# The RWKV stage of a two-stream transformer kernel, with full-width masks, chunks taken by pairs of heads and double buffers

## Chip, cores and metric

The kernel runs on one core of a Trainium2 chip. The time is device microseconds (us) of one execution; lower is better.

## What is computed

The reference runs four transformer layers over a latent and a context stream, 256 tokens of 1024 features each. The first layer's mixer is half attention, half RWKV-7: a linear recurrence for 8 heads of 64, forward (`d` = 0) and backward (`d` = 1) in time, the latent stream starting from the state that the context stream left. Cut to what matters:

```python
kk = kk * lax.rsqrt(jnp.sum(kk * kk, axis=-1, keepdims=True) + EPS)
w_log = w0 + einsum('btdr,drc->btdc', tanh(wl), w2)            # low rank, 64
decay = exp(-exp(-softplus(-w_log) - 0.5))
a = sigmoid(a0 + einsum('btdr,drc->btdc', al, a2))             # low rank, 64
def step(S, inp):
    r, w, k, v, kk, a = inp
    S = (S * w[:, :, None, :]
         - einsum('bhvk,bhk->bhv', S, kk)[..., None] * (kk * a)[:, :, None, :]
         + v[..., None] * k[:, :, None, :])
    return S, einsum('bhvk,bhk->bhv', S, r)
S_cf, y_cf = wkv7_scan(S0, dir_inputs(f_ctx, 0), reverse=False)
_, y_lf = wkv7_scan(S_cf, dir_inputs(f_lat, 0), reverse=False)   # and both backward
```

## The kernel before, in words

Activations lie feature-major: 128 features on the partitions, tokens along the free axis. Big products split each operand in a high and a low fp32r part and take three matmuls (`mm3`, L137); small products are plain fp32. All records of a matmul carry the line of the helper `mm` (L107), so places are told by tile names: `lin` and `aux` are PSUM tiles of big products and attention, `rw` those of the RWKV stage. A scheduler places instructions on each engine's queue in the order that it expects them to become ready, with the order of the code as priority; engines then run their queues in order. PSUM's eight banks are shared by the tags of `BANKS` (L28), which caps `rw` at 5.

The recurrence is done in chunks of 64 tokens (four per stream) and pairs of heads (`hp`, four). Class `Rwkv` (from L878) has, for one stream, generators that yield at their seams: `keys` (key norms and the bonus term), `front` (per pair `features`, then `scores`), `inverse` (a triangular inverse for all pairs at once), `mid` (`chunks`, per pair and per two chunks), `steps` (the state recurrence) and `readout`. `even_mixer` (L702) makes A for the context stream and B for the latent one, and `weave` runs them side by side: A.front with B.keys, A.inverse with the start of B.front, A.mid and A.steps with the rest of it, then A.readout with B.inverse, B.mid, B.steps, B.readout. The output projections (`half_out_proj`) fill in between: `oa` is the attention half, `ob` the RWKV half.

What the change touches:
- `features` (L923): two low rank products of K = 128 and 512 columns (`lowa`, zero-padded so that both directions fit one product), tanh on ScalarE (`FL`, `SA`), then a chain on VectorE with a scan (L941).
- `scores` (L962): transposes of v and Qt (L971, L979); per direction 8 products `ZW`x`SA` into [128, 4, 128], then eight masks on 64 partitions, half into `AL` and half into `BL`; then the products of `BL` and `KV`; then the transposes of `SA` (L1015), copied to `ZW` and `KV` (L1016, L1017); then `KV` products, copied to `Cc` (L1026). `KV` and `BL` have one buffer.
- `chunks` (L1138): 8 products `QV`x`AL`, a copy and a negating copy (L1148 and the next), 28 products, subtractions and additions on VectorE.

```python
                for hf, ps in enumerate(pss):
                    for dst, sr in ((AL[dr, :, hf], slice(0, 64)), (BL[dr, :, hf], slice(64, 128))):
                        m = self.smask[sr, d, None, :].to_broadcast([64, 4, P])
                        self.last_score = k.mul(dst, ps[sr], m)
```

Of the kernel before, what the change touches and what calls it, by code (L numbers as in the profile page):

```python
# [11 lines left out]
AF = mybir.ActivationFunctionType  # L12
# [3 lines left out]
P = 128  # L16
KC = 8
NS = 256
# [9 lines left out]
BANKS = {"lin": 4, "aux": 4, "mod": 1, "rw": 5}  # L28
# [674 lines left out]
def even_mixer(k, nm, gate, nxt):  # L703
# [3 lines left out]
    low = {("gl", s): k.t([P, NS], "low", 1) for s in range(2)}  # L707
    for n in ("wl", "al"):
        for s in range(2):
            low[n, s] = k.t([P, 2, NS], "lowa", 2)  # L710
            for d in range(2):
                k.after(nc.gpsimd.memset(low[n, s][64 - 64 * d:128 - 64 * d, d], 0.0), k.mark)
# [35 lines left out]
    def features():  # L748
        for idx in range(6, 21):
# [4 lines left out]
            for st in sts:  # L754
                if name[0] in "rkv":
                    t = T[name, st.s] = k.t([P, NS], f"rkv{st.s}", 3)
                elif name == "gl":
                    t = low[name, st.s]
                else:
                    t = k.r([P, NS], "s1")  # L760
# [4 lines left out]
                if name in ("wl", "al"):  # L765
                    for d in range(2):
                        dr = slice(64 * d, 64 * d + 64)
                        k.act(low[name, st.s][dr, d], t[dr], AF.Tanh if name == "wl" else AF.Copy)
# [110 lines left out]
class Rwkv:  # L879
# [3 lines left out]
    def __init__(self, k, st, T, low, lora, hb, gw, PCs, msk, before=None):  # L883
        self.k, self.st, self.T, self.low, self.lora, self.hb = k, st, T, low, lora, hb
        self.gw, self.PC, self.before = gw, PCs[st.s], before
        self.rmask, self.smask = msk[:, 0:512], msk[:, 512:768].rearrange("p (d t) -> p d t", d=2)
# [5 lines left out]
    def keys(self):  # L892
# [4 lines left out]
        for hp in range(4):  # L897
            r_, k_, v_ = (T[f"{n}{hp}", st.s] for n in "rkv")
            a = k.r([P, NS], "s1")
            k.stt(a, r_, k.v("r_k", hp), k_, ALU.mult, ALU.mult)  # L900
            pb = rw((P, NS))
            k.mm(pb, k.bd, a, True, True)
            k.mul(bon[:, hp], pb, v_)
            b = k.r([P, NS], "s1")
            k.ts(b, k_, k.v("k_k", hp), ALU.mult, -1.0, ALU.mult)
            sq = k.r([P, NS], "s1")
            k.act(sq, b, AF.Square)
            rr = head_rstd(k, sq, NS, 1.0, 1e-6, "rw")
            k.mul(kks[:, hp], b, rr)
            yield  # L910

    def front(self, early):
# [5 lines left out]
        self.Cc = [k.t([P, 2, 4, 64], "Cc", 4) for _ in range(4)]  # L918
# [3 lines left out]
        def features(hp):  # L922
# [7 lines left out]
            for i, (w, x) in enumerate(((w2, "wl"), (a2, "al"))):  # L930
                pw = rw((P, 2, NS))
                k.mm(pw.rearrange("p d t -> p (d t)"), w[:, cs],
                     self.low[x, st.s].rearrange("p d t -> p (d t)"), True, True)
                for d in range(2):
                    b = 8 * i + 4 * d + hp
                    k.act((SG, A)[i][:, :, d], pw[:, d].rearrange("p (c t) -> p c t", c=4), AF.Tanh, scale=0.5,
# [25 lines left out]
        def scores(hp):  # L962
# [4 lines left out]
            KV = k.t([P, 2, 4, P], "KV", 1)  # L967
# [15 lines left out]
            BL = k.t([P, 4, 2, P], "BL", 1)  # L983
            for d in range(2):
# [6 lines left out]
                for hf, ps in enumerate(pss):  # L991
                    for dst, sr in ((AL[dr, :, hf], slice(0, 64)), (BL[dr, :, hf], slice(64, 128))):
                        m = self.smask[sr, d, None, :].to_broadcast([64, 4, P])
                        self.last_score = k.mul(dst, ps[sr], m)
                yield
            for c in (0, 2):
# [13 lines left out]
                nc.scalar.copy(self.Y[:, hp, 64 * c:64 * c + 128], py.rearrange("p c t -> p (c t)"))  # L1010
            for d in range(2):
# [779 lines left out]
```

## Time and profile before

| | |
|---|---|
| runs | 3443.32 us median of 3 (3440.03 to 3454.67) |
| profiled execution | 3438.3 us, its span 3436.5 us |
| busy | TensorE 94%, VectorE 69%, ScalarE 43% of the span |
| mean granted TensorE clock | 0.961 |
| RWKV stage (about 593 to 953 us in the span) | granted clock 0.59 to 0.83 |

Shares over the whole span say little here: the stage that is changed has its own limits, so it is read by stretches, by the chain of waits within it, and by the timelines of single engines.

### The profile page before, as it was taken

How to read it: one execution, taken by the hardware profiler on the slowest of the kernel's cores; microseconds unless marked ns; L12 is line 12 of the kernel's file. 1: busy time of each engine (PE TensorE's matmuls, PEld its weight loads, DVE VectorE, ACT ScalarE, POOL GpSimd, SP SyncE). 2: the span in 40 equal slices, each digit the busy share in tenths (PEclk: the TensorE clock that was granted, in tenths of full speed). 3: DMA queues.
4: the chain of work that ended last, by engine and by line, in shares of the span. 5: the costliest groups of instructions: out<-in, count | busy, mean ns of one | idle time of the engine just before them, and what ended most of it. 6: DMA issues, size and time to landing. Idle time of an engine off the chain costs nothing.

```text
span 3436.5 us, 51379 instructions
## 1 busy us (share of the span) xinstructions
PE 3239.4 (94%) x20538; PEld 2775.9 (81%) x20538; DVE 2367.3 (69%) x4452; ACT 1489.2 (43%) x2611; POOL 7.1 (0%) x20
## 2 busy tenths in 40 slices
PE   8999989657689999999988999999999999999998
PEld 5888967546578888888878998877888888988998
DVE  6776567676787777587886575653469766755776
ACT  4222366544342224322376445643344335554554
POOL 0000000000000000000000000000000000000000
PEclk9999999757799999999999999999999999999999
DMA  7554211000135554555533532222235542334553
GB/s 278 195 196 145 86 56 57 1 1 20 52 128 196 196 193 169 202 191 192 188 121 130 182 126 79 70 76 84 95 122 196 196 170 100 102 117 164 182 180 103
DMA packets 138256, 458.35 MB, mean 133 GB/s; under 512 B 14368, under 2 KB 20000, under 8 KB 137632
## 3 DMA queue, kind: packets, MB, share of 16 engines
q1 hardware_dynamic: 137152, 451.21, 37.7%
q10 hardware_dynamic: 864, 3.85, 0.3%
q8 instruction: 161, 2.64, 0.3%
q14 instruction: 79, 0.65, 0.1%
HBM read 453.96 MB, written 1.05 MB: 132 GB/s over the span
## 4 chain that ended last, share of the span: by engine, by line
PE 87%; DVE 6%; ACT 4%; DMA 2%; issue 1%; SPq 0%; DVEq 0%; ACTq 0%
PE lin L107 73%; PE aux L107 9%; PE rw L107 4%; PE aux L607 1%; DVE arena L171 1%; DVE arena L153 1%; DMA raw<-in_w_modp 1%; ACT arena L174 1%; DVE inv L153 0%; ACT e L174 0%; DVE SA L153 0%; ACT PT L608 0%; DVE BL L153 0%; DMA raw<-in_ffn_in 0%; DVE wf L153 0%
## 5 line engine op out<-in xcount | busy, mean ns | idle before, releaser
L107 PE MATMUL lin<-h,wf 128*128 128x512 f32 (+1 forms) x6240 | 1173.3, 350 | 0.0
L107 PEld LDWEIGHTS lin<-h,wf 128*128 128x128 f32 x6240 | 1015.5, 189 | 154.1 <-issue 0.8
L177 ACT CAST wf<-raw 128x1024 fp32r<-128x1024 f32 (+1 forms) x412 | 416.2, 1021 | 513.8 <-PE lin L107 405.1
L107 PE MATMUL lin<-hid,wf 128*128 128x512 f32 (+1 forms) x3456 | 614.4, 339 | 0.0
L107 PEld LDWEIGHTS lin<-hid,wf 128*128 128x128 f32 x3456 | 539.6, 190 | 72.4 <-DVE hid L153 0.8
L276 DVE CUSTOM_DVE_ANT_0 prod<-rawd,crow,modc 128x1024 f32<-128x1024 f32 x384 | 481.3, 1280 | 169.4 <-DMA rawd<-in_w_modv 166.0
L153 DVE TENSOR_TENSOR wf<-raw,wf 128x1024 fp32r<-128x1024 f32 (+1 forms) x412 | 488.3, 1187 | 67.7 <-ACT wf L177 65.6
L107 PE MATMUL lin<-h,w 128*128 128x512 f32 (+1 forms) x2328 | 472.8, 358 | 0.7 <-DVE w L153 0.7
L107 PEld LDWEIGHTS lin<-h,w 128*128 128x128 f32 x2328 | 382.0, 190 | 70.3 <-issue 10.0
L171 DVE SCALAR_TENSOR_TENSOR arena<-lin,arena 128x256 f32<-128x256 f32 (+2 forms) x339 | 154.1, 480 | 130.3 <-PE lin L107 95.7
L153 DVE TENSOR_TENSOR w<-raw,w 128x1024 fp32r<-128x1024 f32 x160 | 194.0, 1220 | 71.8 <-ACT w L177 71.1
L107 PE MATMUL aux<-h,w 128*128 128x256 f32 x1632 | 218.7, 295 | 24.1 <-ACT h L174 23.1
L107 PEld LDWEIGHTS aux<-h,w 128*128 128x128 f32 x1632 | 210.7, 201 | 34.5 <-ACT h L174 28.7
L177 ACT CAST hid<-fs 128x512 fp32r<-128x512 f32 (+1 forms) x132 | 72.5, 549 | 262.9 <-DVE fs L153 262.3
L177 ACT CAST w<-raw 128x1024 fp32r<-128x1024 f32 x160 | 165.5, 1048 | 40.5 <-DMA raw<-in_ffn_in 8.9
L174 ACT ACTIVATE arena<-arena 128x256 f32<-128x256 f32 (+1 forms) x269 | 102.0, 393 | 128.0 <-DVE arena L171 86.0
L153 DVE TENSOR_TENSOR fs<-fs,lin 128x512 f32<-128x512 f32 (+1 forms) x80 | 49.7, 621 | 122.0 <-PE lin L107 121.9
L171 DVE SCALAR_TENSOR_TENSOR fs<-lin,arena,fs 128x510 f32<-128x510 f32 (+1 forms) x160 | 98.0, 613 | 22.7 <-ACT fs L174 20.5
L107 PE MATMUL lin<-br,w 128*128 128x512 f32 (+1 forms) x576 | 113.4, 341 | 0.1
L107 PEld LDWEIGHTS lin<-br,w 128*128 128x128 f32 x576 | 89.4, 189 | 15.8 <-issue 4.3
L107 PE MATMUL lin<-w,h 128*128 128x256 f32 x768 | 100.2, 287 | 0.0
L174 ACT ACTIVATE fs<-lin,arena 128x512 f32<-128x512 f32 (+1 forms) x80 | 53.7, 671 | 106.5 <-PE lin L107 106.4
(250 smaller groups left out, 3178.6 us busy)
## 6 DMA issues: line engine op xcount, KB each, us to landing
rawd<-in_w_modv SPq DMA_DIRECT2D x224, 512.0 KB, 4.3
raw<-in_ffn_in SPq DMA_DIRECT2D x176, 512.0 KB, 4.1
raw<-in_w_up SPq DMA_DIRECT2D x88, 512.0 KB, 3.7
raw<-in_ffn_out SPq DMA_DIRECT2D x64, 512.0 KB, 6.3
raw<-in_w_g SPq DMA_DIRECT2D x48, 512.0 KB, 3.6
raw<-in_w_in SPq DMA_DIRECT2D x40, 512.0 KB, 3.6
raw<-in_w_down SPq DMA_DIRECT2D x32, 512.0 KB, 4.6
raw<-in_ffn_out SPq DMA_DIRECT2D x32, 384.0 KB, 4.3
```

The costliest lines, as they stand in the source:

```text
L107: i = self.nc.tensor.matmul(out, lhsT=l, rhs=r, start=start, stop=stop)
L153: return self.nc.vector.tensor_tensor(out, a, b, op=op)
L171: return self.nc.vector.scalar_tensor_tensor(out, a, s, b, op0=op0, op1=op1)
L174: return self.nc.scalar.activation(out, a, f, **kw)
L177: self.after(self.nc.scalar.copy(hi, src), after)
L276: nc.vector.tensor_tensor_reduce(k.t([P, 1024], "prod", 1), raw, rows[s], 1.0, k.modb[:, g, c, s:s + 1], op0=ALU.mult, op1=ALU.add, accum_ ...
L607: k.nc.tensor.transpose(pt[:, kc], e[:, kc * P:(kc + 1) * P], k.ident)
```

## The change

Masks: the scores of both directions are put on one tile, direction on the partitions, so that a mask covers 128 partitions; the products become 64 x 64 tiles, twice as many. The transposes of `SA` and their copies stand ahead of the `BL` products. `KV` and `BL` get two buffers, `rw` six banks. `Cc` is laid out by direction. `chunks` takes a whole pair of heads: 16 products, two copies (no negated copy; the sums downstream change sign), 56 products, wider VectorE instructions. `mid` still yields eight times. The low rank products are taken with K = 64, 256 columns, one per direction, row tile and bank, without zero padding. `keys` works on two pairs at once and has two steps in place of four. The order in which `even_mixer` calls the generators is unchanged.

```diff
-BANKS = {"lin": 4, "aux": 4, "mod": 1, "rw": 5}
+BANKS = {"lin": 4, "aux": 4, "mod": 1, "rw": 6}
...
-    low = {("gl", s): k.t([P, NS], "low", 1) for s in range(2)}
-    for n in ("wl", "al"):
-        for s in range(2):
-            low[n, s] = k.t([P, 2, NS], "lowa", 2)
...
+    low = {(n, s): k.t([P, NS], "low", 2) for n in ("gl", "wl", "al") for s in range(2)}
...
-        for hp in range(4):
-            r_, k_, v_ = (T[f"{n}{hp}", st.s] for n in "rkv")
-            a = k.r([P, NS], "s1")
...
-            rr = head_rstd(k, sq, NS, 1.0, 1e-6, "rw")
-            k.mul(kks[:, hp], b, rr)
+        for q in range(2):
+            a, b = (k.r([P, 2, NS], "s2") for _ in range(2))
...
+            rr = head_rstd(k, a.rearrange("p i t -> p (i t)"), NJ, 1.0, 1e-6, "rw")
+            k.mul(kks[:, 2 * q:2 * q + 2], b, rr.rearrange("p (i t) -> p i t", i=2))
             yield
...
-            for i, (w, x) in enumerate(((w2, "wl"), (a2, "al"))):
-                pw = rw((P, 2, NS))
-                k.mm(pw.rearrange("p d t -> p (d t)"), w[:, cs],
-                     self.low[x, st.s].rearrange("p d t -> p (d t)"), True, True)
+            pws = [rw((P, 2, NS)) for _ in range(2)]
+            k.run([(pws[d][:, i], w[64 * d:64 * d + 64, cs], self.low[x, st.s][64 * d:64 * d + 64], True, True)
+                   for i, (w, x) in enumerate(((w2, "wl"), (a2, "al"))) for d in range(2)])
...
-            KV = k.t([P, 2, 4, P], "KV", 1)
+            KV = k.t([P, 2, 4, P], "KV", 2)
...
-            BL = k.t([P, 4, 2, P], "BL", 1)
-            for d in range(2):
+            BL = k.t([P, 4, 2, P], "BL", 2)
+            for i, dst in enumerate((AL, BL)):
                 pss = [rw((P, 4, P)) for _ in range(2)]
                 for c in range(4):
-                    for hf, ps in enumerate(pss):
-                        hr = slice(64 * hf, 64 * hf + 64)
-                        k.mm(ps[:, c], SA[hr, c, d].rearrange("p i t -> p (i t)"), ZW[hr, c, d], True, True)
+                    for d in range(2):
+                        for hf, ps in enumerate(pss):
+                            hr = slice(64 * hf, 64 * hf + 64)
+                            k.mm(ps[64 * d:64 * d + 64, c], SA[hr, c, d, i], ZW[hr, c, d], True, True)
+                for hf, ps in enumerate(pss):
+                    self.last_score = k.mul(dst[:, :, hf], ps, self.smask[:, None, :].to_broadcast([P, 4, P]))
+                yield
+            for d in range(2):
                 dr = slice(64 * d, 64 * d + 64)
...
+                pt = rw((P, 4, P))
+                for c in range(4):
+                    nc.tensor.transpose(pt[:, c], SA[:, c, d].rearrange("p i t -> p (i t)"), k.ident)
+                nc.scalar.copy(ktok[dr], pt[64:128])
+                nc.scalar.copy(ZW[dr, :, :, 0:64], pt[0:64].rearrange("p c (h t) -> p c h t", h=2))
...
-                for c in range(4):
-                    nc.scalar.copy(self.Cc[c][:, d, hp], pc[d][:, c])
+                nc.scalar.copy(self.Cc[d][:, :, hp], pc[d])
...
     def mid(self):
         for hp in range(4):
-            for c in (0, 2):
-                self.chunks(hp, c)
-                yield
+            yield from self.chunks(hp)
...
-        Hs, NG = (k.r([P, 2, 2, 64], "s1") for _ in range(2))
-        nc.scalar.copy(Hs, pg[:, :, :, 0])
-        k.act(NG, pg[:, :, :, 1], AF.Copy, scale=-1.0)
...
+            HN.append(k.r([P, 2, 2, 2, 64], "s2"))
+            nc.scalar.copy(HN[-1], pg)
+        yield
...
-            for cc in range(2):
-                k.add(Cc[c + cc][:, d, hp], Cc[c + cc][:, d, hp], pz[:, cc, 2])
...
+        for d in range(2):
+            k.sub(Cc[d][:, :, hp], Cc[d][:, :, hp], pcs[d][:, 0])
```

How this moves instructions shows at three places. TensorE in A.front, the third pair of heads before (`BL` and `KV` products, L1015 transposes of `SA`):

```order
L107 MATMUL rw_5163<-KV_5085,BL_5114 64x64 x3
L107 MATMUL rw_5164<-BL_5114,KV_5085 64x64
L107 MATMUL rw_5179<-KV_5085,BL_5114 64x64 x3
L107 MATMUL rw_5180<-BL_5114,KV_5085 64x64
L107 MATMUL rw_5163<-KV_5085,BL_5114 64x64 x5
L107 MATMUL rw_5164<-BL_5114,KV_5085 64x64 x3
L107 MATMUL rw_5179<-KV_5085,BL_5114 64x64 x5
L107 MATMUL rw_5180<-BL_5114,KV_5085 64x64 x3
L1015 MATMUL rw_5195<-arena,SA_4871 128x128 x4
L1015 MATMUL rw_5202<-arena,SA_4871 128x128 x4
L107 MATMUL rw_5209<-KV_5085 64x64 x8
```

and the same place in the change, from the last of the scores (`ZW`, `SA`) on:

```order
L107 MATMUL rw_5146<-ZW_4851,SA_4849 64x128
L107 MATMUL rw_5147<-ZW_4851,SA_4849 64x128
L990 MATMUL rw_5166<-arena,SA_4849 128x128 x4
L990 MATMUL rw_5173<-arena,SA_4849 128x128 x4
L107 MATMUL rw_5180<-KV_5073,BL_5105 64x64 x2
L107 MATMUL rw_5181<-BL_5105,KV_5073 64x64
L107 MATMUL rw_5196<-KV_5073,BL_5105 64x64 x2
L107 MATMUL rw_5197<-BL_5105,KV_5073 64x64
L107 MATMUL rw_5212<-KV_5073 64x64
```

The transposes of `SA` have moved from behind all `BL` products to ahead of them.

VectorE in A.front where the third pair's features begin (`FL`, the scan, `SA`) and the second pair's first mask (`AL`) stands, before:

```order
L168 TENSOR_SCALAR FL_4872<-FL_4872 128x512
L171 SCALAR_TENSOR_TENSOR arena<-arena 128x256
L941 SCALAR_TENSOR_TENSOR FL_4872<-msk_4545,FL_4872 128x512
L153 TENSOR_TENSOR kks_4856<-arena 128x256
L168 TENSOR_SCALAR SA_4871<-SA_4871 128x8x64
L153 TENSOR_TENSOR ZW_4873<-FL_4872 128x4x64 x2
L153 TENSOR_TENSOR SA_4871<-SA_4871,kks_4552 128x8x64
L153 TENSOR_TENSOR FL_4872<-ZW_4873,FL_4872 128x4x64
L168 TENSOR_SCALAR SA_4871<-SA_4871,arena 128x8x64
L153 TENSOR_TENSOR AL_4901<-rw_4919,msk_4545 64x4x128
```

and in the change (`w` and `rawm` are a weight split of the attention half's projection):

```order
L171 SCALAR_TENSOR_TENSOR arena<-lin_4926,arena 128x256
L153 TENSOR_TENSOR w_5129<-rawm_5126,w_5128 128x1024
L153 TENSOR_TENSOR AL_4881<-rw_4899,msk_4530 128x4x128
L171 SCALAR_TENSOR_TENSOR arena<-rw_4841,arena 128x512
L168 TENSOR_SCALAR FL_4850<-FL_4850 128x512
L171 SCALAR_TENSOR_TENSOR arena<-arena 128x512
L168 TENSOR_SCALAR SA_4849<-SA_4849 128x8x64
L153 TENSOR_TENSOR kks_4831<-arena 128x512
L933 SCALAR_TENSOR_TENSOR FL_4850<-msk_4530,FL_4850 128x512
```

The first mask has moved from nine instructions behind the start of the features to ahead of it, and a weight split stands ahead of both.

ScalarE at the end of B.mid (the copies of `rw` to `arena` are those of `chunks`; the casts are weights of the next feed-forward part, fresh from DMA), before:

```order
L1148 COPY arena<-rw_7468 128x256
L174 ACTIVATE arena<-rw_7468 128x256
L174 ACTIVATE arena<-arena 128x256 x2
L177 CAST w_1080_7825<-raw_7823 128x1024
L1148 COPY arena<-rw_7522 128x256
L174 ACTIVATE arena<-rw_7522 128x256
L174 ACTIVATE arena<-lin_7847,arena 128x256
L177 CAST w_1083_7831<-raw_7829 128x1024
L174 ACTIVATE arena<-arena 128x256
L177 CAST w_1086_7837<-raw_7835 128x1024
L1148 COPY arena<-rw_7573 128x256
L174 ACTIVATE arena<-rw_7573 128x256
```

and in the change:

```order
L1139 COPY arena<-rw_7321 128x512
L1139 COPY arena<-rw_7331 128x512
L174 ACTIVATE arena<-arena 128x256 x2
L1139 COPY arena<-rw_7426 128x512
L177 CAST w_1055_7714<-raw_7712 128x1024
L1139 COPY arena<-rw_7436 128x512
L177 CAST w_1058_7720<-raw_7718 128x1024
L177 CAST w_1061_7726<-raw_7724 128x1024
```

The last copy of `chunks` stands behind one cast where it stood behind three. From B.readout on, the engines' queues hold the same instructions as before.

## Rows read from the trace of the kernel before

**Rows 1.** The page: span, busy times, granted clock in 40 slices.

```profile
span 3436.5 us, 51379 instructions
PE 3239.4 (94%) x20538; PEld 2775.9 (81%) x20538; DVE 2367.3 (69%) x4452; ACT 1489.2 (43%) x2611; POOL 7.1 (0%) x20
PEclk9999999757799999999999999999999999999999
```

**Rows 2.** Stretches: from:to, length, busy PE, PEld, DVE, ACT, POOL, then granted clock.

```profile
593.00:695.00 102.00, 68.64 (x575) 52.74 (x573) 66.10 (x129) 58.63 (x141) 1.33 (x2) 0.73 0.00 1
695.00:755.00 60.00, 30.80 (x398) 22.61 (x400) 50.81 (x112) 26.64 (x57) 0.00 (x0) 0.59 0.01 1
755.00:847.00 92.00, 76.44 (x1139) 63.67 (x1137) 57.44 (x158) 40.80 (x109) 1.11 (x2) 0.76 0.05 15
847.00:899.00 52.00, 23.41 (x115) 16.96 (x112) 47.77 (x111) 17.97 (x27) 0.00 (x0) 0.66 0.02 6
899.00:953.00 54.00, 48.69 (x1082) 43.18 (x1080) 30.96 (x111) 19.09 (x41) 0.00 (x0) 0.83 0.26 90
1000.00:3436.00 2436.00, 2387.23 (x14204) 2091.42 (x14203) 1666.13 (x3000) 1060.26 (x1783) 1.99 (x4) 0.99 0.43 148
```

**Rows 3.** The chain of waits over one pair in A.front: start, us, what.

```profile
614.94 4.40 PE rw L107 x46
619.34 1.06 PE rw L1015 x4
620.42 0.58 ACT ZW L1016
...
622.84 3.14 PE rw L107 x20
626.00 0.47 ACT arena L174
626.50 1.28 ACT L174
...
629.03 0.37 DVE FL L168
...
637.34 0.69 DVE BL L153
```

**Rows 4.** Groups of instructions: xcount, busy us, mean ns, idle before.

```profile
L153 DVE TENSOR_TENSOR BL<-rw,msk 64x512 f32<-64x512 f32 x32 | 22.2, 694 | 0.6
L153 DVE TENSOR_TENSOR SA<-SA,FL 128x512 f32<-128x512 f32 x16 | 10.4, 682 | 0.0
```

**Rows 5.** Timeline of PE: start, us, products in records (two per fp32 product).

```profile
604.27 2.06 PE L107 MATMUL rw<-ZW,SA 64*128 64x128 f32 x32
715.24 3.79 PE L107 MATMUL rw<-ZW,SA 64*128 64x128 f32 x32
754.56 1.97 PE L107 MATMUL rw<-QV,AL 64*64 64x128 f32 x16
782.38 1.04 PE L107 MATMUL rw<-QV,AL 64*64 64x128 f32 x14
747.70 2.08 PE L107 MATMUL rw<-lowa,lora 128*128 128x512 f32 x2
```

**Rows 6.** Waits within the stage: who, for whom, us in total, times, longest.

```profile
PE rw L107 <- DVE BL L153: 30.8, 12, 7.3
PE rw L107 <- ACT arena L1148: 7.6, 11, 1.5
PE rw L107 <- ACT KV L1017: 6.9, 12, 1.4
```

**Rows 7.** Timeline of ScalarE: tanh for B's pairs, and the end of B.mid.

```profile
749.82 0.84 ACT L174 ACTIVATE FL<-rw,arena 128x256 f32<-128x256 f32 x2 [1.03 <-PE rw L107]
787.19 0.84 ACT L174 ACTIVATE FL<-rw,arena 128x256 f32<-128x256 f32 x2 [3.02 <-PE rw L107]
819.76 0.84 ACT L174 ACTIVATE FL<-rw,arena 128x256 f32<-128x256 f32 x2 [5.24 <-PE rw L107]
935.21 1.04 ACT L177 CAST w<-raw 128x1024 fp32r<-128x1024 f32 x1 [2.35 <-DMA raw<-in_ffn_in]
939.75 1.04 ACT L177 CAST w<-raw 128x1024 fp32r<-128x1024 f32 x1 [0.22 <-DMA raw<-in_ffn_in]
940.70 0.37 ACT L1148 COPY arena<-rw 128x256 f32<-128x256 f32 x1
```

More of the change, by code (lines that the diff above doesn't have):

```diff
@@ L764, in features @@
                 k.stt(t[:, :-1], ps[:, o + 1:o + NS], k.v("mu", 15 + ci), t[:, :-1], ALU.mult, ALU.add)
[L765 to L768, printed above, removed]
+                if name == "wl":
+                    k.act(t, t, AF.Tanh)
                 elif name == "gl":
@@ L917, in front @@
         self.AL, self.QV, self.ZW = {}, {}, {}
-        self.Cc = [k.t([P, 2, 4, 64], "Cc", 4) for _ in range(4)]
+        self.Cc = [k.t([P, 4, 4, 64], "Cc", 4) for _ in range(2)]
         self.Y = k.t([P, 4, NS], "Y", 2)
@@ L1136, in inverse, with chunks @@
             yield
-    def chunks(self, hp, c):
+    def chunks(self, hp):
         k, nc, rw = self.k, self.k.nc, self.rw
         AL, QV, ZW, Cc = self.AL[hp], self.QV[hp], self.ZW[hp], self.Cc
-        pg = rw((P, 2, 2, 2, 64))
-        for cc in range(2):
+        HN = []
+        for c in (0, 2):
+            pg = rw((P, 2, 2, 2, 64))
+            for cc in range(2):
+                for hf in range(2):
+                    for d in range(2):
+                        dr = slice(64 * d, 64 * d + 64)
+                        k.mm(pg[dr, cc, hf], AL[dr, c + cc, hf, 0:64], QV[dr, c + cc, :, 64 * hf:64 * hf + 64],
+                             True, True)
+            HN.append(k.r([P, 2, 2, 2, 64], "s2"))
+            nc.scalar.copy(HN[-1], pg)
+        yield
+        pzs = [rw((P, 4, 2, 64)) for _ in range(2)]
+        pcs = [rw((P, 2, 4, 64)) for _ in range(2)]
+        for c in range(4):
@@ L1160, in chunks @@
-        py = rw((P, 2, 64))
-        for cc in range(2):
+                    b_ = ZW[dr, c, hf, 0:64]
+                    k.mm(pzs[d][hr, c, 0], hn[dr, 0], AL[dr, c, hf, 64:128], True, True)
+                    k.mm(pzs[d][hr, c, 1], hn[dr, 0], b_, True, True)
+                    k.mm(pcs[d][hr, 0, c], b_, hn[dr, 1], True, True)
+        for c in range(4):
             for hf in range(2):
                 hr = slice(64 * hf, 64 * hf + 64)
-                k.mm(py[hr, cc], NG[:, cc, hf], AL[:, c + cc, hf, 64:128], True, True)
+                k.mm(pcs[0][hr, 1, c], HN[c // 2][:, c % 2, hf, 1], AL[:, c, hf, 64:128], True, True)
@@ L1165, in chunks @@
         for d, pz in enumerate(pzs):
[L1166 to L1171 removed]
+            k.sub(ZW[:, :, d, 64:128], ZW[:, :, d, 64:128], pz[:, :, 0])
@@ L1173, in step @@
+            k.sub(ZW[:, :, d, 0:64], k.eye2[:, None, :].to_broadcast([P, 4, 64]), pz[:, :, 1])
+        for d in range(2):
+            k.sub(Cc[d][:, :, hp], Cc[d][:, :, hp], pcs[d][:, 0])
+        yc = self.Y[:, hp].rearrange("p (c t) -> p c t", c=4)
+        k.sub(yc, yc, pcs[0][:, 1])
+        yield
     def step(self, PC, j, last):
@@ L1192, in step @@
             for d in range(2):
-                src = self.Cc[cd[d]][:, d]
+                src = self.Cc[d][:, cd[d]]
                 if pS is not None:
@@ L1667, in _consts @@
     s, t = (p % 64)[:, None], (p % 64)[None]
-    half = (p // 64)[None]
+    half, back = (p // 64)[None], (p // 64)[:, None]
     d0 = np.where(half == 0, s < t, s <= t)
     d1 = np.where(half == 0, s > t, s >= t)
-    msk[:, 512:640], msk[:, 640:768] = d0, d1
+    msk[:, 512:640] = np.where(back == 0, d0, d1)
     for j in range(4):
```

71 lines of the change are left out of this document (22 added, 49 removed).

## The prediction

> **What bounds the kernel now.** The page comes first: TensorE is busy for 94% of the span and its granted clock is low only in seven or eight of forty slices, those of the RWKV stage [rows 1]. The table of stretches says the same in numbers: from 1000 us to the end TensorE is busy for 2387 of 2436 us at clock 0.99, while in the five stretches from 593 to 953 us no engine is full and the clock lies between 0.59 and 0.83 [rows 2]. The change touches only this stage, and behind it the queues are as before, so the question is how much of these 360 us is waiting that goes away. The chain of waits over one pair in A.front shows a loop through three engines [rows 3]: `BL` products 4.4 us, transposes of `SA` 1.06, four copies of 0.58 on ScalarE, `KV` and key products 3.14, a table load either side of a reciprocal root (1.28, 0.47, 1.28), and only at 629.0 the next features on VectorE, whose last seven masks begin at 637.3 and last about 0.7 each, until the next `BL` products at 641. That is 26 us for a pair, while VectorE in this stretch is busy for 66 of 102 us and TensorE for 69, at 0.73 of its clock [rows 2]. The list of waits has the same edges: TensorE waited 30.8 us for masks, 6.9 for the `KV` copies and 7.6 for the copies of `chunks` [rows 6]. So it is latency that bounds the stage, and shorter links count.
>
> **The change, per pair of heads (eight pairs).**
> - Masks: eight of 64 partitions become four of 128. The mask takes 694 ns on 64 partitions, and a multiplication of the same 512 columns on 128 takes 682 [rows 4], so 5.6 us become 2.8: -2.8, on the path wherever TensorE waits for `BL`.
> - Transposes of `SA` and their copies, 1.06 + 4 x 0.58 = 3.4 us, stand ahead of the `BL` products and run while VectorE masks: -3.4. The cover is the time of the masks and of the next features; without it they cost what they did.
> - Low rank products: two records took 2.08 us at the low clock, so a pair's four take 4.2 there and half of it at the high one [rows 5]. Of K = 64 there are eight of 256 columns in two row tiles. The scores, which before alternate two row tiles, give the rate: a lone record of 128 columns would take a quarter of the low rank one (0.26 at the low clock), they take 3.79 / 32 = 0.12 [rows 5]. Taken two at a time they halve: -1.0 to -2.1, taken as -1.
> - Scores: 32 records become 64 of 64 x 64. The nearest row is `QV`x`AL`, the same tile and column count, alternating two tiles: 1.97 / 16 = 0.123 us at the low clock, 1.04 / 14 = 0.074 at the high one [rows 5]. 64 of these make 7.9 and 4.8 us against 3.79 and 2.06: +4.1 and +2.7. If all four tiles run at once the bound is nothing: 64 records in the time of 32. I take +1.5, since half of the products stand behind the first mask's inputs and run beside the masks. The Trainium skill, TensorEngine Tiling (Array Packing), Key Properties, says that different tiles load and multiply in parallel, by which this term would be nothing and the sum below -52 in place of -40; the rows by themselves would make it -19 to -30. The same section says that a change of tiling mode drains TensorE, which speaks against the change (the low rank products now switch mode too); no row shows a drain apart from the rest, and the sum has nothing for it.
> - `chunks`: per pair two waits of TensorE for the copy (7.6 / 11 = 0.7 each [rows 6]) fall behind other products: -1.2. Wider VectorE instructions save it some 2 us per pair, off the path. Second buffers and the sixth bank cost nothing by themselves.
>
> **The sum.** Gross, about 3.4 + 2.8 + 1 = 7 us for a pair, 5.7 with the scores.
> 1. A.front, three steps from pair to pair: the first gains nothing. In the new order a weight split, its cast (1.04 us) and a mask stand ahead of the third pair's features, and the mask waits for low rank, transposes and half of the scores, about 627 + 4 us against the 629 at which these features began. The other two gain 5 each, one table load pair falling away in the last: -10 (0 to -20).
> 2. A.inverse: VectorE alone is the path (busy 50.8 of 60 us [rows 2]). B's first pair loses 2.8 us of masks there and the last quarter of B's keys, six instructions of some 0.4: -5 (-3 to -7). The recursion itself is untouched.
> 3. Behind it TensorE runs the 32 x 32 products with the low rank ones between: -2 (0 to -2).
> 4. A.mid with B's other three pairs: tanh of one pair to the next takes 37.4 and 32.6 us [rows 7]. 5.7 + 1.2 less some cover makes 6.3 each: -19 (0 to -34).
> 5. B.inverse and A.readout: unchanged, 0.
> 6. B.mid: the last copy of `chunks` came at 940.70, after three casts that waited for DMA from 935.21 on [rows 7]; now it waits for one. The first DMA keeps its place, tied to a matmul about three quarters through B.mid: -4 (0 to -7). What is late next is that first cast.
> Sum -40: 3438.3 becomes 3398 for the profiled execution. That execution lies 5 us under the median of the runs shown, 3443.3, so for a median **3403 us**.
>
> **Rivals.**
> - *The rest of the waiting goes too, and TensorE keeps its clock.* In 755 to 847 us it was busy 76.4 us at 0.76 [rows 2]; at 0.95 the same work takes 61, 15 us more than I count, and A.front, with VectorE as its bound (some 8 us of features and 2.8 of masks a pair, against 20 in my sum), could give 10 more. -65: 3378. For it: the work between idle gaps is denser; the clock is 0.99 wherever TensorE is dense [rows 2]. The Trainium skill, TensorE: Matmul & The Clock Gate, section on HAM oscillation, says that idle gaps throttle the clock again, by which fewer gaps would give this case; the rows agree (0.59 where it is busy half the time). Against it: the wait for features remains in each pair. 20%.
> - *The moved waits come back.* If TensorE runs 755 to 847 us at 0.6, as in the stretch before it [rows 2], its work there grows from 76 to 97 us and eats term 4; with a first mask that stalls VectorE in every pair of A.front only 12 us are left: 3431. The wait of the mask ahead of the features is the place to look. 13%.
> - *Small tiles run one after the other.* At the low rank rate a lone record of 128 columns takes 0.13 us at the high clock and 0.26 at the low one; 64 of them make 8.3 and 16.6 us, 6.3 to 12.8 more than before, about 77 us in eight pairs against a gross gain of 52: +25, 3468, slower. It decides from 52 / 8 = 6.5 us more per pair, that is some 0.15 us a record. Against it: `QV`x`AL` runs at 0.074 to 0.123 [rows 5]. 4%.
> - *Part of it doesn't happen.* "Keys of both streams first" is no new order of calls: keys merely takes two steps, so that B's last keys move from A.inverse to A.front. Without that, 2.5 us of term 2 stay: 3406, within the forecast.
>
> **How the numbers follow.** The forecast, -20 to -55, gets 63%. A measurement of this kernel can tell about 0.5%, 17 us, from no change. Faster by more: the forecast, the first rival and a part of the second, 0.87; within: the rest of the second and the weak end of the forecast, 0.09; slower 0.04. The range leaves out the third rival, and a little at either end: 3366 takes in the first rival with the page's price for the scores, 3428 a sum of -15, terms 1 and 4 near their poor bounds.
>
> **What would show it.** Right: masks of 128 x 512 at about 0.69 us, sixteen for `AL` and sixteen for `BL`; 64 score records in 2 to 5 us at the high clock; the wait of TensorE for `BL` masks (30.8 us) down by half; the wait for the `KV` copies near nothing; tanh of B's pairs 26 to 31 us apart; the stretch from the start of the inverse to the end of B.mid shorter by 30 us, and everything from the next feed-forward part on shifted, not changed. Wrong: scores over 6.5 us longer; features that begin only after a mask that VectorE waited for, pair after pair; a clock near 0.6 through A.mid; or a stage as long as before because the first weights of the next part arrive late.

## The result, and the profile after

The changed kernel takes 3365.65 us (median of 4 runs, 3363.35 to 3368.72) against 3444.74 us of the kernel before, measured beside it: ratio 0.9767, 95% interval 0.9743 to 0.9791, a gain of 79 us. The prediction was 3403 us, a gain of 40, with a range down to 3366, just above what was measured: right in direction, half the size. A second comparison of the same two kernels (p17 below) gave 0.9774 (0.9761 to 0.9788).

The page after the change, beside [rows 1]:

```profile
span 3366.1 us, 51619 instructions
PE 3196.4 (95%) x20810; PEld 2745.1 (82%) x20810; DVE 2333.3 (69%) x4320; ACT 1473.3 (44%) x2525; POOL 4.5 (0%) x12
PEclk9999999877899999999999999999999999999999
```

The RWKV stage shrank, nothing else: from the first state sum of B.steps (945.1 us before, 873.4 after) to the end of the span, which takes in the last row of [rows 2], both kernels take 2491 to 2493 us. To compare stages whose starts have shifted, I cut them at events on VectorE: the first scan, the first transpose of A's inverse, the first transpose behind A's recursion, the same two of B, and the first state sum of B.steps. So the stretches are A.front, A.inverse, the tail of the inverse with A.mid and A.steps, B.inverse with A.readout, and B.mid (columns as in [rows 2]). Before:

```profile
596.89:694.31 97.42, 64.75 (x564) 50.84 (x562) 62.38 (x123) 54.51 (x135) 1.33 (x2) 0.72 0.00 1
694.31:734.85 40.54, 18.96 (x134) 14.04 (x134) 38.04 (x94) 13.60 (x34) 0.00 (x0) 0.63 0.00 1
734.85:847.51 112.66, 88.79 (x1409) 72.74 (x1411) 70.90 (x177) 54.94 (x135) 1.11 (x2) 0.71 0.04 15
847.51:890.53 43.02, 22.74 (x99) 16.29 (x95) 39.47 (x104) 10.19 (x17) 0.00 (x0) 0.70 0.01 3
890.53:945.11 54.58, 43.39 (x922) 38.31 (x922) 31.37 (x98) 26.39 (x51) 0.00 (x0) 0.76 0.24 82
```

and after:

```profile
593.07:664.13 71.06, 56.46 (x720) 41.52 (x718) 53.84 (x112) 52.43 (x107) 1.25 (x2) 0.92 0.03 9
664.13:698.05 33.92, 10.99 (x156) 9.15 (x156) 32.31 (x83) 10.72 (x24) 0.00 (x0) 0.55 0.01 1
698.05:779.06 81.01, 65.20 (x1458) 57.65 (x1458) 55.80 (x115) 51.12 (x107) 1.11 (x2) 0.80 0.05 15
779.06:826.67 47.61, 24.97 (x152) 18.40 (x152) 42.01 (x111) 11.46 (x20) 0.00 (x0) 0.71 0.03 12
826.67:873.36 46.69, 36.97 (x915) 35.01 (x916) 26.32 (x51) 22.06 (x36) 0.00 (x0) 0.78 0.24 80
```

A.front lost 26 us and A.mid 32. In A.front TensorE issues more records and is busy for 8 us less, at clock 0.92 where it had 0.72. B.inverse became 5 us longer: two state sums of A.steps now run inside it (780.23 and 784.29 us), where before it was one (848.68 us). The chain of waits over the third pair in A.front (pieces left out at the dots) replaces [rows 3]:

```profile
623.48 1.14 DVE FL L933
...
627.27 0.60 DVE AL L153
627.87 0.60 DVE FL L153
628.62 0.60 DVE BL L153
629.26 1.72 PE rw L107 x28
630.99 0.66 PE lin L107 x2
631.65 3.32 PE rw L107 x59
634.97 0.45 ACT FL L174
```

From features to the next pair's tanh are 11.5 us; transposes, their copies and the `KV` wait have left the chain over this pair. Over the first and the last pair they are still on it (transposes at 604.93 and 655.11 us, copies behind them). The timeline of TensorE, beside [rows 5]:

```profile
600.23 1.98 PE L107 MATMUL rw<-ZW,SA 64*64 64x128 f32 x64
641.02 2.66 PE L107 MATMUL rw<-ZW,SA 64*64 64x128 f32 x64
613.09 0.70 PE L107 MATMUL rw<-KV 64*64 64x64 f32 x32
616.62 1.13 PE L107 MATMUL rw<-low,lora 64*128 64x256 f32 x8
```

So 64 score records take the time of 32 before (2.06 us), both at the full clock: four quarters of the array at once, which p11 below tests. The second row, 2.66 us, is one at a mean clock of 0.73. The groups of the masks, as [rows 4]:

```profile
L153 DVE TENSOR_TENSOR AL<-rw,msk 128x512 f32<-128x512 f32 x16 | 10.5, 685 | 9.9 <-PE rw L107 9.9
L153 DVE TENSOR_TENSOR BL<-rw,msk 128x512 f32<-128x512 f32 x16 | 10.5, 681 | 0.0
```

The waits within the stage: that for `BL` masks fell from 30.8 us [rows 6] to 3.2, and one that was there all along is now first, that behind the recursions. Before (L1110 is the copy that is L1098 after):

```profile
PE rw L107 <- ACT inv L1110: 26.4, 2, 17.7
```

and after:

```profile
PE rw L107 <- ACT inv L1098: 34.2, 2, 17.5
PE rw L971 <- DVE FL L153: 18.5, 3, 14.0
PE rw L107 <- DVE BL L153: 3.2, 4, 1.8
```

And tanh of B's pairs, 37.4 and 32.6 us apart in [rows 7], is 22.5 and 22.8 apart:

```profile
712.14 0.47 ACT L174 ACTIVATE FL<-rw,arena 128x256 f32<-128x256 f32 x1 [0.83 <-PE rw L107]
734.62 0.47 ACT L174 ACTIVATE FL<-rw,arena 128x256 f32<-128x256 f32 x1 [0.47 <-PE rw L107]
757.37 0.47 ACT L174 ACTIVATE FL<-rw,arena 128x256 f32<-128x256 f32 x1 [0.47 <-PE rw L107]
```

### The profile page after: what moved, and what is told of

Its sections match the earlier page's. It is cut to its first block, busy times and chain, and to the rows that moved or that the text cites. A ratio compares the mean times of both kernels' runs of the same rounds, so it can differ in the third digit from the quotient of the medians.

```text
span 3366.1 us, 51619 instructions
## 1 busy us (share of the span) xinstructions
PE 3196.4 (95%) x20810; PEld 2745.1 (82%) x20810; DVE 2333.3 (69%) x4320; ACT 1473.3 (44%) x2525; POOL 4.5 (0%) x12
## 4 chain that ended last, share of the span: by engine, by line
PE 76%; DVE 7%; ACT 4%; DMA 2%; issue 1%; DVEq 0%; ACTq 0%; SPq 0%
PE lin L107 64%; PE aux L107 8%; PE rw L107 3%; DVE arena L171 1%; PE aux L607 1%; DVE arena L153 1%; DMA raw<-in_ffn_in 1%; ACT arena L174 1%; DVE inv L153 0%; ACT e L174 0%; ACT PT L608 0%; DMA raw<-in_w_up 0%; DVE SA L153 0%; DVE wf L153 0%; DVE ZW L153 0%
## 5 line engine op out<-in xcount | busy, mean ns | idle before, releaser
L171 DVE SCALAR_TENSOR_TENSOR arena<-lin,arena 128x256 f32<-128x256 f32 (+1 forms) x331 | 150.4, 480 | 119.5 <-PE lin L107 98.6
L174 ACT ACTIVATE arena<-arena 128x256 f32<-128x256 f32 (+2 forms) x261 | 100.7, 399 | 106.7 <-DVE arena L171 87.9
L171 DVE SCALAR_TENSOR_TENSOR fs<-lin,arena,fs 128x510 f32<-128x510 f32 (+1 forms) x160 | 98.0, 613 | 22.8 <-ACT fs L174 20.6
L174 ACT ACTIVATE fs<-lin 128x512 f32<-128x512 f32 (+1 forms) x80 | 43.2, 541 | 152.7 <-PE lin L107 144.5
```

The lines of the kernel that those rows point to most:

```text
L171: return self.nc.vector.scalar_tensor_tensor(out, a, s, b, op0=op0, op1=op1)
L174: return self.nc.scalar.activation(out, a, f, **kw)
```

## The experiments

All in one table: ratio to the kernel before with its interval, then us and granted clock of three stretches in the one profile of each (A.mid stands for the third stretch; all are cut as above). The expectations name theories by letters. L is the prediction's: each link that falls away gives its own length. C: behind a wait TensorE runs at half clock, and a shorter wait spares that too. S: pairs overlap only by the second buffers and the sixth bank. K: `keys` are the hidden link. J: the parts pay only together.

| run | ratio | A.front | A.mid | B.mid |
|---|---|---|---|---|
| before | 1 | 97.4, 0.72 | 112.7, 0.71 | 54.6, 0.76 |
| p9 before again | 1.0006 (0.9994–1.0019) | 101.2, 0.66 | 112.2, 0.71 | 57.3, 0.72 |
| p1 masks | 0.9947 (0.9932–0.9962) | 91.9, 0.72 | 110.0, 0.72 | 57.1, 0.72 |
| p2 transposes | 0.9909 (0.9891–0.9927) | 89.6, 0.74 | 100.5, 0.79 | 56.1, 0.72 |
| p3 buffers | 0.9987 (0.9976–0.9999) | 104.0, 0.67 | 108.3, 0.79 | 58.6, 0.71 |
| p5 keys | 0.9970 (0.9957–0.9983) | 104.7, 0.72 | 112.6, 0.70 | 53.7, 0.75 |
| p6 low rank | 0.9985 (0.9975–0.9996) | 100.6, 0.67 | 111.9, 0.68 | 56.4, 0.72 |
| p7 mid | 0.9919 (0.9901–0.9937) | 101.1, 0.66 | 100.8, 0.81 | 46.0, 0.79 |
| p13 `KV` order | 0.9997 (0.9984–1.0011) | 101.5, 0.66 | 115.5, 0.68 | 57.1, 0.74 |
| p8 = p1+p2+p3 | 0.9849 (0.9831–0.9867) | 76.8, 0.84 | 95.2, 0.82 | 54.3, 0.75 |
| p4 dummies, A.front | 0.9956 (0.9941–0.9971) | 92.1, 0.96 | 114.6, 0.71 | 53.9, 0.75 |
| p14 dummies, mid | 0.9969 (0.9955–0.9984) | 101.5, 0.66 | 104.4, 0.84 | 53.1, 0.81 |
| after | 0.9767 (0.9743–0.9791) | 71.1, 0.92 | 81.0, 0.80 | 46.7, 0.78 |
| p17 after again | 0.9774 (0.9761–0.9788) | 69.9, 0.94 | 81.1, 0.79 | 48.8, 0.78 |
| p10 old mid | 0.9815 (0.9787–0.9843) | 71.7, 0.90 | 93.7, 0.75 | 54.9, 0.76 |
| p15 old transposes | 0.9838 (0.9814–0.9861) | 86.7, 0.80 | 88.8, 0.77 | 48.4, 0.78 |
| p11 one tile | 0.9824 (0.9804–0.9843) | 73.1, 0.95 | 95.5, 0.73 | 47.8, 0.79 |
| p12 dummies, inverse | 0.9750 (0.9728–0.9772) | 70.0, 0.93 | 79.2, 0.85 | 46.0, 0.89 |
| p16 inverse tail | 0.9749 (0.9733–0.9765) | 69.8, 0.95 | 79.4, 0.81 | 46.7, 0.79 |
| p18 p16 + dummies | 0.9779 (0.9766–0.9793) | 78.5, 0.91 | 79.7, 0.83 | 44.3, 0.84 |

**The parts alone.** Each is a hunk of the change on the kernel before. p1, the scores' loop with its mask constant:

```diff
-            for d in range(2):
+            for i, dst in enumerate((AL, BL)):
```

> The kernel before with one part of the change: scores as 64x64 products and masks on 128 partitions. Theory L (the prediction's: each link of the loop that falls away gives its own length, at the clock that the stretch has): 2.8 us less per pair, 1.5 given back by twice as many products, so about -10 us in all, A.front -4. Theory C (behind each long wait for the masks TensorE runs at half clock, and a shorter wait spares that too): -15 to -25, with fewer stretches at clock 0.5 in A.front. Theory S (pairs overlap only because of the second buffers and the sixth bank): about -5, since the next link waits for the single buffers. The 64 score records: 2.0 us at the high clock if four tiles run at once, 4 or more if not.

p2, the transposes and their copies ahead of the `BL` products:

```diff
+            for d in range(2):
+                dr = slice(64 * d, 64 * d + 64)
+                pt = rw((P, 4, P))
...
             for c in (0, 2):
                 pb = rw((P, 2, P))
```

> The kernel before with one part: the transposes of SA and their four copies ahead of the BL products. Theory L: 3.4 us per pair, -20 us in all, of it -9 to -10 in A.front. Theory C: the wait for the masks is filled by only 1 us of transposes and stays, so the half clock behind it stays: no more than L, -20. Theory S: -5 to -10, the copies into the one KV buffer waiting for the pair before.

p3:

```diff
-BANKS = {"lin": 4, "aux": 4, "mod": 1, "rw": 5}
+BANKS = {"lin": 4, "aux": 4, "mod": 1, "rw": 6}
...
-            KV = k.t([P, 2, 4, P], "KV", 1)
+            KV = k.t([P, 2, 4, P], "KV", 2)
...
-            BL = k.t([P, 4, 2, P], "BL", 1)
+            BL = k.t([P, 4, 2, P], "BL", 2)
```

> The kernel before with one part: KV and BL with two buffers, six rw banks. Theory L: 0 (-3 to +3). Theory C: 0 to -3. Theory S: -10 or more, as the next pair's masks and copies no longer wait for the products of the pair before.

p5 takes `keys`, p6 the low rank products with their tiles `low`:

```diff
-        for hp in range(4):
+        for q in range(2):
```

```diff
-                pw = rw((P, 2, NS))
...
+            pws = [rw((P, 2, NS)) for _ in range(2)]
```

> The kernel before with one part: keys on two pairs at once, two steps in place of four. In A.front each step of B's keys puts a product, a reciprocal root and two table loads of 1.28 us between the copies of one pair and the features of the next. Theory L (as predicted): -5 in all, of it -2.5 in A.inverse, A.front -2.5. Theory K (keys are the hidden link of A.front): A.front -8 to -12 by itself and the first scan some 4 us earlier, -15 in all. Theory J (parts pay only together, each alone moving the wait to the next link): -3 to -6.

> The kernel before with one part: low rank products of K = 64 in two row tiles, no zero padding. Theory L: -1 per pair, -6 to -8 in all at most, 0 where they run ahead of need (A.front). Theories J and K: -2 to -5.

p7 takes `chunks`, `mid`, the layout of `Cc` and the `KV` products' order; p13 of these the order alone:

```diff
-            for d in range(2):
-                for c in range(4):
-                    for hf in range(2):
+            for c in range(4):
+                for hf in range(2):
+                    for d in range(2):
```

> The kernel before with one part: chunks for a whole pair of heads, Cc by direction, KV products in the order chunk, head half, direction. Theory L: -1.2 per pair in A.mid, -4 in B.mid, -8 to -9 in all. The rival to it, that the KV products in four quadrants run at twice the rate (32 records 0.7 us against two halves of 0.68) and the wider VectorE instructions (2 us per pair) lie on the path: B.mid -8, A.mid -8 to -10, -16 to -18 in all. Five rw banks for a step that wants six may also hold it back: 0.

> The kernel before with one line of the mid part: the KV products in the order chunk, head half, direction (four quarters of the array in turn) in place of one direction after the other. If this order is the hidden half of the mid part: 32 records in 0.7 us in place of two halves of 0.68 and a wait of 0.5 between them, -0.7 to -1.2 us a pair, -6 to -10 us in all, ratio 0.997 to 0.998. If the products now all wait for the last copy of KV, which came between the halves before: 0, ratio 0.999 to 1.001.

By 3448 us the six measured 18, 31, 4, 10, 5 and 28 us; the product of their ratios is 0.9720, 97 us. Theory L holds in kind (parts give something alone, so S falls), but not in size: masks 18 for 10, transposes 31 for 20, mid 28 for 9. The 18 lie where C put the masks (15 to 25); the 31 and the 28 lie above every forecast made for them (C gave the transposes 20 at most). The two buffers alone are at the edge of what can be told. Of K, the first scan came 3.4 us earlier, counted from the last projection of r, k, v, but A.front was no shorter; `keys` gave 10 us, between L's 5 and K's 15. Of p7, A.mid fell by 11.9 us and B.mid by 8.6 to 11.3, at a higher clock; the `KV` order is none of it (p13), since `KV` products there still wait for two copies one after the other.

p8:

> The kernel before with three parts together: masks, transposes ahead, second buffers with six banks. Alone they measured 0.9947, 0.9909 and 0.9987. Theory L (they add): 0.984, -54 us, A.front -7 from its first scan to the start of the inverse (97.4 us before). Theory J (together they close the waits, and the clock stays up): below 0.982, A.front -18 or more, with the clock above 0.82 there.

0.9849 is the product of the three (0.9844): they add, L. Within A.front, though, J's sign is there: 76.8 us at 0.84, at least 20 us less than before, where the three alone give 12 by their profiles (against the mean of the two of before). Two profiles of one kernel differ there by 4 us, as the next shows, so the sign is larger than that; over the whole kernel it isn't seen. p9:

> The kernel before, once more, for a second profile of it. If the profile shown of it was a fast one of its kind (its 3438.3 us lie 9 us under the median of 3447.6 on the chip of the first four experiments), A.front, from its first scan to the start of the inverse, takes 100 to 106 us here in place of 97.4, at a lower clock, and the other stages the same within 1 us: unchanged A.front code took 100.6 and 101.1 us in the low rank and mid experiments. If the parts alone had lengthened A.front there, it takes 97 to 98 again. The ratio to itself should be 1.000.

A.front took 101.2 us at 0.66, as expected; B.mid also took 2.7 us more, which was not. The profile that the prediction worked from was a short execution: its stage is 373.0 us from the last projection of r, k, v to the first state sum of B.steps, here 380.6.

**The clock.** p4 changes no work:

```diff
+                            if early and c + cc + hf == 0:
+                                for _ in range(((9, 24, 9, 4), (9, 9, 22, 10))[d][hp]):
+                                    k.mm(pb[:, d], k.ident, k.ident, True, True)
                             k.mm(pb[dr, cc, hc], BL[dr, c + cc, hf, 0:64], VV[dr, c + cc, hc], True, True)
```

> The kernel before, unchanged in its work, with dummy products (identity by identity, 128 columns, into a place that is overwritten afterwards) ahead of the first and the second BL product of each of the four pairs of A.front, 9/24/9/4 and 9/9/22/10 of them, sized to the waits for masks there. Theory C: the clock stays at 1.0 through A.front in place of 0.5 behind each wait, so about 8 to 10 us at half clock per pair shrink by 4 to 5: -12 to -18 us, all of it before the inverse. Theories L and S: 0, or slower by the part of the dummies that outlasts a wait (0 to +8).

Measured -15 us (-20 to -10) by the ratio, C. Stretches of 5 us around the first pair, before:

```profile
605.00:610.00 5.00, 4.72 (x38) 3.68 (x36) 4.98 (x12) 2.21 (x4) 0.00 (x0) 1.00 0.00 0
610.00:615.00 5.00, 0.35 (x4) 0.25 (x4) 4.88 (x9) 0.20 (x1) 0.00 (x0) 0.83 0.02 3
615.00:620.00 5.00, 5.00 (x50) 4.18 (x51) 4.53 (x10) 1.28 (x4) 0.00 (x0) 0.50 0.00 0
620.00:625.00 5.00, 4.52 (x41) 3.63 (x40) 0.00 (x0) 3.85 (x13) 0.00 (x0) 0.50 0.00 0
```

and with the dummies, where the same products follow the second and third pair's masks:

```profile
640.00:645.00 5.00, 5.00 (x63) 3.85 (x64) 1.81 (x4) 2.93 (x7) 0.00 (x0) 1.00 0.01 3
660.00:665.00 5.00, 4.64 (x71) 4.25 (x69) 3.78 (x7) 1.19 (x4) 0.00 (x0) 1.00 0.00 0
```

TensorE idles in 610 to 615 us, and the ten busy us behind it run at the lower of its two levels, 0.50; with the dummies only the first pair still shows some of it (0.72 to 0.94 in 610 to 625 us), the other three run at 1.00. The eight records of a pair's transposes show what that is worth, before at 0.50 and with the dummies at 1.00 (first pair before, second pair of p4):

```profile
619.27 1.97 PE L1015 MATMUL rw<-arena,SA 128*128 128x128 f32 x8
```

```profile
642.62 1.09 PE L1018 MATMUL rw<-arena,SA 128*128 128x128 f32 x8
```

One other thing changes in p4: the scheduler puts projection products (`lin`), of which 14 records stood at 606.25 us before, ahead of the first pair's wait, behind it (10 of them at 626.50 us). So the work is held fixed, but not the order of the queue. p14 puts dummies into A.mid, B.mid and B's pairs of the kernel before:

```diff
+        for _ in range(2):
+            k.mm(pzs[0].rearrange("p a b t -> p (a b t)")[:, 0:P], k.ident, k.ident, True, True)
         for d, pz in enumerate(pzs):
```

> The kernel before with dummy products of 128 columns on TensorE: two ahead of each group of chunk products, where it waits some 0.5 us for their copies, and eight ahead of the BL products of B's pairs. No work is changed. Theory C (the half clock behind short waits makes A.mid and B.mid long): the clock of A.mid rises from 0.71 to 0.85 or more, A.mid falls from 112.5 to 100 to 106 us, B.mid by 2 to 5, -8 to -15 in all. If the stage is paced by VectorE and ScalarE: 0, or +2 to +6 where dummies outlast the waits.

Measured -11 us (-16 to -6), the clock of A.mid up to 0.84: C again. In A.mid the dummies alone give 8 of the 12 us that p7 gives, in B.mid some 3 of 10: with the clock as high as in p7 (0.81 and 0.79), the larger share there is by elimination the merged copies and wider VectorE instructions (26.3 us busy in B.mid after, 31.4 before), which no run separates.

**Parts undone, from the changed kernel.** p10 has the old `chunks`, p15 the old place of the transposes (the hunks of p7 and p2 with + and - exchanged).

> The changed kernel with the old chunks, Cc and copies of Cc (the KV products keep their new order). If the mid part is worth as much at the end as alone (0.9919): 28 us slower than the changed kernel, 0.985 of before, B.mid 54 us in place of 46.7 and A.mid 10 us longer. If the parts overlap (the six measured alone make 0.972 as a product, the changed kernel 0.977), here is where they do: 0.981 to 0.983.

> The changed kernel with the transposes of SA and their copies back behind the BL products. Alone the move was worth 31 us (0.9909). If it is worth as much within the rest: 0.985 of before, A.front 78 to 80 us in place of 71.1 and A.mid 92 in place of 81. If it is here that the parts overlap, because wider masks leave less of a wait to hide the transposes in: 0.981 to 0.983.

Within the rest the mid part is worth 14 to 17 us (28 alone) and the transposes 22 to 24 (31 alone), each uncertain by 8 to 10: enough for the 17 us by which 97 exceeds the measured 80. p10 bears its second forecast out; p15's interval takes in both of its own. p15 brings back two waits, named so in its list:

```profile
PE rw L107 <- DVE BL L153: 14.7, 7, 4.2
PE rw L107 <- ACT KV L1007: 9.2, 14, 1.4
```

p11 keeps four score products on one quarter:

```diff
-                for c in range(4):
-                    for d in range(2):
-                        for hf, ps in enumerate(pss):
+                for hf, ps in enumerate(pss):
+                    for d in range(2):
+                        k.run([(ps[64 * d:64 * d + 64, c], SA[hr, c, d, i], ZW[hr, c, d], True, True)
+                               for c in range(4)])
```

> The changed kernel with the score products in another order: four successive ones on the same quarter of the array, before the next quarter. If a quarter's products run one after the other and different quarters at the same time, 64 records take 6 to 8.3 us at the high clock in place of 1.98 (by the low rank row before, 128 columns 0.13 us each), that is 4 to 6 us more for a pair, +25 to +45 us in all: about 0.985 to 0.990 of before. If the rate of a record is set by its columns alone whatever the tile: 1.98 us and no change, 0.977.

```profile
598.90 4.63 PE L107 MATMUL rw<-ZW,SA 64*64 64x128 f32 x64
```

4.63 us at the full clock against 1.98, less than the 6 expected, and 17 to 20 us in all: the order of the loops alone is worth as much as the masks. Most of it shows in A.mid, 95.5 us at 0.73 for 81.0 at 0.80; A.front grew by 2 to 3 us only.

**What is left.** p12 puts 25 dummies behind each recursion, the first of which reads its last product:

```diff
+            if hh == 0:
...
+                for x in [tmp[:, 0:31]] + [k.ident] * 24:
...
+                        i = nc.tensor.matmul(pf[:, 0:x.shape[-1]], lhsT=k.ident, rhs=x, start=True, stop=True)
```

p16 has the transposes for the 32x32 products first, copied to two tiles of their own:

```diff
+        XR = [k.r([P, 2, 8, 32], "s2") for _ in range(2)]
...
-        for d in range(2):
-            qr = slice(64 * d, 64 * d + 64)
-            nc.vector.transpose(XT[qr], (rows, cols)[d](X[qr]))
         for q, f in ((0, cols), (3, rows)):
...
+        for d in range(2):
+            qr = slice(64 * d, 64 * d + 64)
+            nc.vector.transpose(XT[qr], (rows, cols)[d](X[qr]))
```

p18 has p16 with ten dummies behind each recursion, nine in the third pair of A.front and seven in the first:

```diff
+                for _ in range(7 if early and hp + d == 0 else 0):
+                    k.mm(pt[:, 3], k.ident, k.ident, True, True)
```

p17, beside it, is the changed kernel once more.

> The changed kernel with 25 dummy products on TensorE in each of the two inverses, from the end of the recursion (the first reads its last result) to the first 32x32 product, 8.3 us in which TensorE is idle there. Theory C: the 15 and 12 us at half clock that follow (706 to 721, 835 to 847 us) run at the full one: -3 to -6 each, -6 to -12 in all, 0.973 to 0.975 of before. If these stretches are paced by the copies on ScalarE between the 32x32 products, nothing: 0.977. If the dummies outlast the wait: +1 to +4.

> The changed kernel with another end of the inverse: the transposes for the 32x32 products first (their copies go to tiles of their own, half by half), the transposes and copies of the diagonal blocks behind. TensorE waits 34.2 us for the copies there (all in the two inverses), some 8.3 us from the end of a recursion. Latency theory: the first 32x32 product starts 3 to 4 us earlier in each inverse, and as the copies of the diagonal blocks are then late next, 2 to 3 us each reach the end: -4 to -7 us, ratio 0.975. Rival: VectorE and ScalarE have the same copies to do before the second products, so nothing is won: 0.977.

> The changed kernel once more, as the measure for p18 on the same chip, and for a second profile of it: 0.9767 of before if the first comparison holds. The spread of its times is 5 us (3363.35 to 3368.72) where that of before is 15 to 20: if the spread of before comes from the clock in A.front (97.4 and 101.2 us in its two profiles), A.front, now at clock 0.92, takes 70 to 72 us here, within 1 us of 71.1, and the whole stage 301 to 303.

> The changed kernel with the end of the inverse of p16 and with dummy products in its remaining waits: 7 ahead of the first pair's transposes of SA, 9 behind the third pair's transposes of v, 9 behind the end of each recursion. If both kinds of loss are still there and add: -6 to -10 us against p17, 0.974 of before, A.front 68 to 70, A.mid 77 to 79. If the clock falls again at the 32x32 products as it did at 706.5 us with 25 dummies ahead of them, and A.front is now paced by VectorE: no more than p16, -3 to -5, 0.975.

By their ratios p12 and p16 came out 6 to 9 us below the two measurements of the changed kernel, and the difference of two such ratios is uncertain by 7 to 11 us: a gain is likely, but not shown. In p12 the mean clock of B.mid rose from 0.78 to 0.89, and B.mid took 46.0 us for 46.7 and 48.8: a higher mean clock is not time by itself. In p16 the wait fell from 34.2 us to

```profile
PE rw L107 <- ACT arena L1096: 25.4, 4, 12.6
```

yet A.mid became shorter by 1.6 us only and B.mid by nothing: ScalarE's copies of the diagonal blocks (5.0 us from 699.05 us on) now stand ahead of the copies that the second 32x32 products read, for which TensorE waits 1.4 us. p18 gained nothing:

```profile
602.43 3.36 PE L107 MATMUL rw<-arena 128*128 128x128 f32 x14 [4.14 <-DVE AL L153]
```

Seven products meant to fill 2 us took 3.4 on the path of the first pair, at a granted clock of 0.63 in 600 to 605 us: dummies that come behind a wait run at the lower level themselves. And the wait ahead of them is 4.14 us where it is 2.07 in p17: the scheduler moved other work with them. The second pair's scan starts 5.5 us behind the first, where it is 7.3 in p17, and projection products that stand around that wait in p17 (`lin`, 2 records at 599.46 us and 8 at 602.67) come later. A.front grew to 78.5 us, so p18 doesn't tell whether dummies could help that wait. No version was shown to be faster than the changed kernel; p16 is the lowest, 3360.4 us.

## Why the prediction was right in direction and half the size

Against the mean of two profiles on each side (stretches as above, "keys" from the last projection of r, k, v to the first scan):

| term | predicted | measured |
|---|---|---|
| keys ahead of the first scan | 0 | -3.4 |
| 1 A.front | -10 | -28.8 |
| 2 A.inverse | -5 | -6.6 |
| 3, 4 tail and A.mid | -21 | -31.4 |
| 5 B.inverse, A.readout | 0 | +4.2 |
| 6 B.mid | -4 | -8.2 |

The direction, the place and most signs of "what would show it" came as written: masks of 0.68 us, the `BL` wait gone, everything behind the stage unchanged. What failed:

- **The per-pair prices, and with them terms 1 and 4, took the clock of the stretch as given.** They valued a link that falls away at its length at 0.59 to 0.83 of the clock [rows 2], and left the remaining products at their half-clock lengths. p4 and p14 show that the half clock behind the waits was itself worth 15 and 11 us (7 and 11 by the profiles), without any work removed. The change raised the clock of A.front from 0.72 to 0.92 and of A.mid from 0.71 to 0.80, and these terms (4 with 3) measured 29 and 31 us in place of 10 and 21. This was the first rival, given 20%: its 3378 us lie nearer than the forecast's 3403, and its claim on TensorE's clock came true in A.front, in A.mid only in part (it put 0.95 there). The section on HAM oscillation of the Trainium skill's page TensorE: Matmul & The Clock Gate, which that rival cited, says that gaps in TensorE's work throttle its clock again; p4 and p14 agree (0.50 behind the gap of 610 to 615 us, 1.00 in p4's second to fourth pair; 0.71 and 0.84 in A.mid).
- **The scores' +1.5 a pair was nothing.** 64 records take 1.98 us and 32 took 2.06; p1 gave 18 us: with the 1.5 eight pairs come to 10, without it to 22. The Trainium skill, TensorEngine Tiling (Array Packing), Key Properties, said so (tiles work in parallel); the trace agrees for four tiles (31 ns a record), and p11 adds that it needs successive products on different tiles (72 ns a record). By that rule alone the sum would have been -52.
- **`chunks` at -1.2 a pair was too small**: 3.5 alone, 2 within the rest. The 2 us of VectorE time that it "saves off the path" were probably in part on it, in B.mid above all: p14's dummies give only some 3 of the 10 us there, and no run tells the wider instructions from the merged copies.
- **"The first gains nothing"** (term 1) was wrong: features of the third pair began at 621.5 us against 629.0 [rows 3]. Half of these 7.5 us lies ahead of the first scan (593.1 us for 596.9), so the step itself gained 3.7. The mask ahead of them did come first in the queue and waited 1.8 us, but the low rank products that start its chain ran at 616.6 us, where I had put them at about 627. VectorE after:

```profile
619.63 0.69 DVE L153 TENSOR_TENSOR AL<-rw,msk 128x512 f32<-128x512 f32 x1 [1.78 <-PE rw L107]
621.53 0.42 DVE L168 TENSOR_SCALAR FL<-FL 128x512 f32<-128x512 f32 x1
```

- Term 2 held. The transposes' 3.4 us a pair are 3.9 alone (31 us) and about 3 within the rest; alone, the clock of A.mid rose to 0.79 with them, so the 31 us are not the link's length only. Keys alone were worth 10 us, where p5's expectation puts the prediction's share at 5: 3.4 of it ahead of the first scan, where no term stood. Term 5 missed the state sum that moved into B.inverse, 2.1 us of VectorE; the rest of the +4.2 was not followed up.

Since the parts overlap by 17 us, these corrections don't simply add up to the 39 us missed. How they share it, and how much of it is the clock's in the changed kernel, stays open: p4 and p14 measured the clock's share in the kernel before, each by itself.

## What to carry to other kernels

Where TensorE's clock is low in a stretch that waits, price a shorter wait twice: the link itself, and half the length of the busy products right behind it; a kernel with dummy products in the wait measures the second share, as long as they don't displace other work (p4's did a little, p18's more). Count products on different tiles as simultaneous only as far as a row shows it: four 64x64 tiles in turn took 31 ns a record, two in turn 74 (`QV`x`AL` [rows 5], 14 records), four successive products on one tile 72. So look at the order of the loops before the number of products. And take the length of a stage from two profiles: executions of one kernel can differ there (97.4 and 101.2 us for A.front) by as much as a term of the sum.

## What the runs showed of the hardware that I had not expected

In p12 the dummies raised the clock behind the recursion, but, after a wait of 0.83 us, it fell again while TensorE was busy without a gap, with 32x32 products and the low rank ones among them:

```profile
700.00:705.00 5.00, 4.17 (x59) 3.98 (x60) 4.88 (x7) 4.46 (x5) 0.00 (x0) 0.99 0.00 0
705.00:710.00 5.00, 5.00 (x178) 4.15 (x172) 1.71 (x6) 3.65 (x8) 0.00 (x0) 0.69 0.01 3
710.00:715.00 5.00, 5.00 (x96) 4.03 (x94) 4.62 (x9) 4.11 (x13) 0.00 (x0) 0.50 0.02 5
```

What TensorE did before and during the fall, in the timeline:

```profile
704.57 2.12 PE L107 MATMUL rw<-inv,AL 32*32 32x32 f32 x122 [0.83 <-ACT inv L1098]
708.56 1.91 PE L107 MATMUL rw<-AL,inv 32*32 32x32 f32 x62
```

So being busy in the record does not by itself keep the higher level. And the times of the kernel before spread over 20 us (3438 to 3458 on one chip, 15 runs), those of p4 and of the changed kernel over 5 to 6 (3433 to 3439 and 3363 to 3369, 4 runs each). That the clock makes this spread is not borne out: p3, at a clock of 0.67 in A.front, spread over 5 us in ten runs, and p10, at 0.90, over 19 in four. What makes it stays open.
